# Compressed keys, values and queries as products in three rows, and a different bank for the first compressed scores

## The chip, the cores and the metric

The kernel runs on one core of a Trainium2 chip. The metric is the device time of one execution in microseconds. Before the change it is 561.64 us, the median of three runs (560.61 to 561.91).

## The reference, cut to what matters

One decoder layer: a Conformer convolution module beside native sparse attention, cross-attention, a SwiGLU network, all in float32, 256 positions of width 1024. What the change touches is the compressed branch of the attention:

```
kc = h @ w_in[kc], vc = h @ w_in[vc]          # (S, 4 groups, 64)
q  = h @ w_in[q]                              # (S, 16 heads, 64)
z  = blocks(kc) + pos                         # blocks of 32 positions, stride 16: 15 of them
k_cmp = silu(einsum("bnlgd,lde->bnge", z, w1)) @ w2
s_c   = q . k_cmp * scale + bias              # masked softmax over the 15 blocks
```

The sum over `l, d` is linear, so the positions' own share, `einsum(pos, w1)`, is one vector of 64 numbers that is the same for every block and group. `v_cmp` is made in the same way from `vc`. Beside it, a depthwise convolution with 31 taps runs over 1024 channels.

## The kernel before, in words

Weights come from DRAM in chunks of 128 x 8 x 256 floats, each in two halves of 128 x 1024, in the order u0 to u7, kc, vc, q0 to q3, ks, kw, vs, vw, ga0 to ga3, gc0 and so on. There are two ways to multiply with a chunk.

`gemm` (line 250) splits each half of the weights in two with `split` (line 170): ACT copies it to a rounded high part (line 174), and DVE subtracts that from it to get the low part (line 175). PE then makes three products for each block (`rows`, line 228): high weights by high activations, high by low, low by high, in this order, each a row of eight matmuls. So a half needs its high part first and its low part only for the third row. The raw half lies in one of four buffers ("w"), the high part in one of five, the low part in one of five. `whole` (line 260) takes the raw float32 weights and the float32 activations `hf` in one float32 matmul for each block; the profile shows each of these as two records. Before the change kc, vc and q0 to q3 go through `whole`, and the chunks around them through `gemm`.

The convolution's taps are dealt to DVE (`taps_v`, line 394, with sums in the two PSUM buffers called "pt") and to ACT with POOL (`taps_g`, line 409: ACT multiplies into one of four "vw" buffers, POOL adds to `yt`). They are given low priority (line 437) and fill in between the other work. The last taps on DVE write `part67`, and only then are the two "pt" buffers free.

Tile's scheduler writes the final order of every engine's queue at build time. On the chip each engine takes its own queue strictly in that order.

PSUM has the tags "mm" (two buffers), "s" (two), "pt" (two), "o" and "s0". `bank` (line 136) deals chunks to "mm" and "s" in turn. `compressed_scores` (line 673) makes the compressed scores of the two halves of the queries, `cs_ps0` and `cs_ps1`, four heads at a time between the rows of ga1 and ga2, both in "pt"; DVE then adds them to the bias `nsc` (line 682). `scores` (line 707) makes the selected and window scores of two heads: `s1_0` and `s1_1` in "s", `s0_0` in "s0".

For the compressed keys, ACT copies kc out of PSUM into `kvt` (lines 497 to 500, four copies), DVE gathers the blocks and adds the positions into `zins` (line 504), and 32 matmuls reduce `zins` with `w1t` into `z_ps` (line 523), which a sigmoid and two products finish (lines 526 to 534).

Of the kernel before, what the change touches and what calls it, by code (L numbers as in the profile page):

```python
# [97 lines left out]
def tile_hybrid_block(  # L98
# [161 lines left out]
    def whole(name, x):  # L260

        ps = bank(f"ps_{name}")
        for i in range(2):
            w = raw(name, i)
            for k in range(4):
                kb = 4 * i + k
                for b in range(2):
# [1 line left out]
                    mm = nc.tensor.matmul(ps[:, b], lhsT=w[:, k, cs], rhs=x[:, kb], start=kb + b == 0, stop=kb == NB - 1 and b == 1)  # L269
# [221 lines left out]
    nc.vector.memset(zz, 0.0)
    kvt = long("kvt", 11, (P, 2, GROUPS, S))
    zins = long("zins", 13, (P, 2, 16, GROUPS, 16))
    for kv, name in enumerate(("kc", "vc")):
        ps = whole(name, hf)
# [4 lines left out]
        act = nc.scalar.activation(kc[64:128, 1::2, 0:S - 1], ps[64:128, :, 1:S], AF.Copy)  # L500
# [3 lines left out]
        vec = nc.vector.tensor_tensor(
            out=zin[:, :, :, 0:NCMP],
            in0=bass.AP(tensor=view.tensor, offset=view.offset,
                        ap=[list(view.ap[0]), [2, 16], [S, GROUPS], [16, NCMP]]),
            in1=ppt[:, PP_POS + 16 * kv:PP_POS + 16 * kv + 16].unsqueeze(2).unsqueeze(3).to_broadcast(
                [P, 16, GROUPS, NCMP]), op=ALU.add)
# [7 lines left out]
    def hidden():  # L517


        z_ps = aux("z_ps", [P, 64], "o", 1)  # L520
        for l in range(16):
            for kv in range(2):
                nc.tensor.matmul(z_ps[HD * kv:HD * kv + HD], lhsT=w1t[:, kv, l], rhs=zins[:, kv, l].rearrange("p g n -> p (g n)"),
                                 start=l == 0, stop=l == 15)
# [12 lines left out]

# [135 lines left out]
    def compressed_scores():  # L673

        for qb in range(2):
            cs_ps = aux(f"cs_ps{qb}", [P, HEADS, 2, 16], "pt", 2)
            for hd in range(HEADS):
                with in_line():
                    last[:] = [nc.tensor.matmul(cs_ps[:, hd], lhsT=qh(hd, qb), rhs=kcp[:, hd // 4], start=True, stop=True)]
                yield  # L680
            for i in range(2):
                nc.vector.tensor_tensor(out=nsc[:, qb], in0=cs_ps[:, :, i], in1=nsc[:, qb], op=ALU.add)
# [739 lines left out]
```

## Time and profile before

| | |
|---|---|
| median of three runs | 561.64 us |
| profiled execution | 561.33 us |
| its span | 559.4 us |
| PE busy | 549.5 us, 98% |
| PE weight loads busy | 506.4 us, 91% |
| DVE busy | 458.6 us, 82% |
| ACT busy | 377.3 us, 67% |
| POOL busy | 135.5 us, 24% |
| mean granted TensorE clock | 0.996 |

Shares over the whole span hide the stages. POOL works only from 46 to 172 us, where the convolution runs, and for short pieces later. What bounds a stage is read from that stage's rows: which engine has no idle time, and which wait ends last. All times below are from the span's start; 1.93 us of the execution lie outside the span.

### The profile page before, as it was taken

To read this page: it belongs to the slowest core of one execution; us is meant where nothing else is said; L and a number is where in the kernel's file an instruction comes from. 1 tells how busy PE (TensorE), PEld (TensorE's weight loads), DVE (VectorE), ACT (ScalarE), POOL (GpSimd) and SP (SyncE) were. 2 spreads that over 40 slices of the span, in tenths; PEclk is the share of its full clock that TensorE was granted. 3 is DMA by queue.
4 is the path that set the end of the run, shared out by engine and by line. 5 is a ranking of instruction groups with operands and counts; after the bars stand their busy time and mean duration, and the time that the engine had idled before them with its cause. 6 is when DMAs were issued, how large, how long until landed. Compare 5 with 4: busy or idle time off the path is not lost.

```text
span 559.4 us, 10351 instructions
## 1 busy us (share of the span) xinstructions
PE 549.5 (98%) x3880; PEld 506.4 (91%) x3880; DVE 458.6 (82%) x862; ACT 377.3 (67%) x711; POOL 135.5 (24%) x121
## 2 busy tenths in 40 slices
PE   9999999999989999999999999999999999999995
PEld 8999998899979999899999999999888888888884
DVE  3898976899988799795777866486999999899896
ACT  4678648789866688679745675476576666666653
POOL 0006996989992000300002200060000000000000
PEclk9999999999989999999999999999999999999999
DMA  8949714448453544425555742543654665454531
GB/s 307 392 157 337 254 15 123 133 161 267 155 190 103 167 154 131 136 77 163 180 193 179 262 153 77 189 151 117 224 187 158 199 198 197 151 168 173 197 104 75
DMA packets 29153, 97.30 MB, mean 174 GB/s; under 512 B 3120, under 2 KB 5680, under 8 KB 28848
## 3 DMA queue, kind: packets, MB, share of 16 engines
q1 hardware_dynamic: 28384, 95.42, 50.8%
q10 hardware_dynamic: 720, 1.23, 0.6%
q8 instruction: 30, 0.49, 0.4%
q14 instruction: 19, 0.16, 0.1%
HBM read 95.39 MB, written 1.25 MB: 173 GB/s over the span
## 4 chain that ended last, share of the span: by engine, by line
PE 92%; DVE 5%; ACT 1%; issue 1%; DMA 1%; DVEq 0%
PE ps_f L1148 15%; PE ps_u L239 8%; PE ps_f L1150 7%; PE fo L1180 7%; PE ps_q L269 4%; PE ps_pw L239 4%; PE ps_v L239 4%; PE ps_xq L239 4%; PE ps_wo L239 4%; PE ps_xo L239 4%; PE ps_gc L239 4%; PE ps_ga L239 3%; PE ps_k L239 3%; PE m L1180 3%; PE s L718 2%; PE pt_a L763 1%
## 5 line engine op out<-in xcount | busy, mean ns | idle before, releaser
L421 POOL TENSOR_TENSOR yt<-yt,vw 128x512 f32<-128x512 f32 x61 | 94.1, 1544 | 54.9 <-ACT vw L419 51.3
L1148 PE MATMUL ps_f<-g,f_1h 128*128 128x512 f32 x176 | 49.0, 397 | 0.0
L419 ACT ACTIVATE vw<-vt,ppt 128x256 f32<-128x256 f32 x104 | 44.5, 498 | 6.4 <-POOL yt L421 6.3
L1148 PE MATMUL ps_f<-g,f_0h 128*128 128x512 f32 x176 | 48.5, 397 | 0.0
L405 DVE SCALAR_TENSOR_TENSOR yp<-vt,ppt,yp 128x256 f32<-128x256 f32 x108 | 44.3, 480 | 0.2
L1148 PEld LDWEIGHTS ps_f<-g,f_1h 128*128 128x128 f32 x176 | 32.9, 188 | 7.5
L1148 PEld LDWEIGHTS ps_f<-g,f_0h 128*128 128x128 f32 x176 | 30.1, 188 | 4.1
L175 DVE TENSOR_TENSOR f_1l<-f,f_1h 128x1024 fp32r<-128x1024 f32 x22 | 27.5, 1248 | 4.1 <-ACT f_1h L174 2.6
L1150 PEld LDWEIGHTS ps_f<-g,f_0l 128*128 128x128 f32 x176 | 27.0, 189 | 3.8
L269 PE MATMUL ps_q<-hf,q 128*128 128x256 f32 x128 | 28.5, 381 | 0.0
L1150 PE MATMUL ps_f<-g,f_0l 128*128 128x256 f32 x176 | 28.3, 283 | 0.0
L174 ACT ACTIVATE f_1h<-f 128x1024 fp32r<-128x1024 f32 x22 | 23.3, 1057 | 7.4 <-PE ps_xo L239 3.7
L175 DVE TENSOR_TENSOR f_0l<-f,f_0h 128x1024 fp32r<-128x1024 f32 x22 | 26.8, 1218 | 1.7 <-ACT f_0h L174 1.7
L269 PEld LDWEIGHTS ps_q<-hf,q 128*128 128x128 f32 x128 | 24.1, 190 | 3.2
L1150 PE MATMUL ps_f<-g,f_1l 128*128 128x256 f32 x176 | 26.5, 281 | 0.0
L174 ACT ACTIVATE f_0h<-f 128x1024 fp32r<-128x1024 f32 x22 | 23.1, 1050 | 1.3 <-PE ps_xo L239 1.3
L738 ACT ACTIVATE p<-p,mins 128x256 f32<-128x256 f32 x32 | 15.9, 499 | 11.2 <-DVE mins L723 11.2
L1150 PEld LDWEIGHTS ps_f<-g,f_1l 128*128 128x128 f32 x176 | 23.3, 188 | 0.0
L1151 ACT ACTIVATE ab<-ps_f 128x256 f32<-128x256 f32 x44 | 16.5, 375 | 8.7 <-PE ps_f L1150 7.9
L1152 DVE TENSOR_TENSOR ab<-ps_f,ab 128x256 f32<-128x256 f32 x44 | 18.3, 419 | 4.7 <-ACT ab L1151 4.5
L283 ACT ACTIVATE uh<-sl 128x256 fp32r<-128x256 f32 x22 | 9.1, 415 | 15.8 <-DVE sl L1156 15.8
L1155 ACT ACTIVATE sl<-ab 128x256 f32<-128x256 f32 x22 | 9.2, 417 | 13.5 <-DVE ab L1153 13.0
(574 smaller groups left out, 1608.8 us busy)
## 6 DMA issues: line engine op xcount, KB each, us to landing
f<-in_wst_dram SPq DMA_DIRECT2D x44, 512.0 KB, 5.5
fo<-in_wfo_dram SPq DMA_DIRECT2D x22, 512.0 KB, 3.7
u<-in_wst_dram SPq DMA_DIRECT2D x14, 512.0 KB, 5.6
q<-in_wst_dram SPq DMA_DIRECT2D x8, 512.0 KB, 5.4
ga<-in_wst_dram SPq DMA_DIRECT2D x8, 512.0 KB, 4.2
gc<-in_wst_dram SPq DMA_DIRECT2D x8, 512.0 KB, 4.5
v<-in_wst_dram SPq DMA_DIRECT2D x8, 512.0 KB, 4.7
pw<-in_wst_dram SPq DMA_DIRECT2D x8, 512.0 KB, 3.8
```

Source lines behind the costliest of these rows:

```text
L174: copy = nc.scalar.activation(hi, w, AF.Copy)
L175: splits[name] = copy, nc.vector.tensor_tensor(out=lo, in0=w, in1=f(hi[:]), op=ALU.subtract)
L239: mm = nc.tensor.matmul(ps[:, b], lhsT=lhsT, rhs=rhs, start=row + b + kb == 0, stop=kb == NB - 1 and row == 2 and b == 1)
L269: mm = nc.tensor.matmul(ps[:, b], lhsT=w[:, k, cs], rhs=x[:, kb], start=kb + b == 0, stop=kb == NB - 1 and b == 1)
L405: nc.vector.scalar_tensor_tensor(out=out[:, i] if t == ts[-1] else acc[i], in0=v, scalar=w, in1=acc[i], op0=ALU.mult, op1=ALU.add)
L419: nc.scalar.activation(pr[:, i], v, AF.Identity, scale=w, bias=col(PP_DB, j + i) if t == 0 else 0.0)
L421: nc.gpsimd.tensor_tensor(out=y, in0=y, in1=pr, op=ALU.add)
L1148: nc.tensor.matmul(ps, lhsT=hs[kb // 4][0][:, kb % 4, cs], rhs=fg[:, :, kb], start=kb == 0, stop=False)
L1150: nc.tensor.matmul(ps[:, 1], lhsT=hs[kb // 4][1][:, kb % 4, cs], rhs=fg[:, 0, kb], start=False, stop=kb == NB - 1)
L1151: nc.scalar.activation(ab[:, b], ps[:, 0], AF.Copy)
L1152: nc.vector.tensor_tensor(out=ab[:, b], in0=ps[:, 1], in1=ab[:, b], op=ALU.add)
L1180: mm = nc.tensor.matmul(o, lhsT=a[x], rhs=b[w], start=start and n == 0, stop=stop and n == 2)
```

## The change

The chunks kc, vc and q0 to q3 go through `gemm` in place of `whole`. kc and vc are kept in two tiles of five groups: four hold the keys or values, the fifth is zero except for the sixteen positions of a sub-row, which DVE copies there. The 32 matmuls read the blocks straight out of these tiles with a stride of 16 positions, 75 columns (5 groups by 15 blocks) where they were 64. The fifth group's column is the positions' share; ACT copies it to `at`, and it enters as the sigmoid's bias and as a scalar in the two products. `zins` is gone. `cs_ps0` lies in "s", `cs_ps1` stays in "pt".

```diff
-    in_order = CHUNKS[CHUNK_AT["ks"]:CHUNK_AT["pw0"]]
+    in_order = CHUNKS[CHUNK_AT["kc"]:CHUNK_AT["pw0"]]
...
-    kvt = long("kvt", 11, (P, 2, GROUPS, S))
-    zins = long("zins", 13, (P, 2, 16, GROUPS, 16))
+    kvt = [long(f"{n}t", slot, (P, GROUPS + 1, S)) for n, slot in (("k", 11), ("v", 13))]
     for kv, name in enumerate(("kc", "vc")):
-        ps = whole(name, hf)
-        kc = kvt[:, kv]
-        nc.scalar.activation(kc[0:64, 0::2, :], ps[0:64], AF.Copy)
...
-        zin = zins[:, kv]
-        nc.vector.memset(zin[:, :, :, NCMP:], 0.0)
-        view = kc
-        vec = nc.vector.tensor_tensor(
-            out=zin[:, :, :, 0:NCMP],
-            in0=bass.AP(tensor=view.tensor, offset=view.offset,
-                        ap=[list(view.ap[0]), [2, 16], [S, GROUPS], [16, NCMP]]),
-            in1=ppt[:, PP_POS + 16 * kv:PP_POS + 16 * kv + 16].unsqueeze(2).unsqueeze(3).to_broadcast(
-                [P, 16, GROUPS, NCMP]), op=ALU.add)
+        ps = gemm(name, h)
+        kc = kvt[kv]
+        nc.scalar.activation(kc[0:64, 0:GROUPS:2, :], ps[0:64], AF.Copy)
...
+        nc.vector.memset(kc[:, GROUPS], 0.0)
+        vec = nc.vector.tensor_copy(kc[:, GROUPS, 0:32:2], ppt[:, PP_POS + 16 * kv:PP_POS + 16 * kv + 16])
         convolve(10 - 2 * kv, 5, act, vec)
...
-        z_ps = aux("z_ps", [P, 64], "o", 1)
+        z_ps = aux("z_ps", [P, GROUPS + 1, NCMP], "o", 1)
         for l in range(16):
             for kv in range(2):
-                nc.tensor.matmul(z_ps[HD * kv:HD * kv + HD], lhsT=w1t[:, kv, l], rhs=zins[:, kv, l].rearrange("p g n -> p (g n)"),
+                nc.tensor.matmul(z_ps[HD * kv:HD * kv + HD], lhsT=w1t[:, kv, l], rhs=kvt[kv][:, :, 2 * l:2 * l + 16 * (NCMP - 1) + 1:16],
                                  start=l == 0, stop=l == 15)
-        zs = small("zs", [P, 64], tag="zs", bufs=2)
-        sig = nc.scalar.activation(zs, z_ps, AF.Sigmoid)
+        zs = small("zs", [P, GROUPS, NCMP], tag="zs", bufs=2)
+        at = small("at", [P, 1])
+        nc.scalar.activation(at, z_ps[:, GROUPS, 0:1], AF.Copy)
+        sig = nc.scalar.activation(zs, z_ps[:, :GROUPS], AF.Sigmoid, bias=at)
...
-        nc.vector.tensor_tensor(out=zz[:HD, 0, :64], in0=z_ps[:HD], in1=zs[:HD], op=ALU.mult)
-        nc.vector.tensor_tensor(out=zs[HD:], in0=z_ps[HD:], in1=zs[HD:], op=ALU.mult)
+        nc.vector.scalar_tensor_tensor(out=z1, in0=z_ps[:HD, :GROUPS], scalar=at[:HD], in1=zs[:HD], op0=ALU.add, op1=ALU.mult)
+        nc.vector.scalar_tensor_tensor(out=zs[HD:], in0=z_ps[HD:, :GROUPS], scalar=at[HD:], in1=zs[HD:], op0=ALU.add, op1=ALU.mult)
...
     for j in range(4):
-        ps = whole(f"q{j}", hf)
+        ps = gemm(f"q{j}", h)
...
-            cs_ps = aux(f"cs_ps{qb}", [P, HEADS, 2, 16], "pt", 2)
+            cs_ps = aux(f"cs_ps{qb}", [P, HEADS, 2, 16], ("s", "pt")[qb], 2)
```

The scheduler's order moves with it, from the chunk u7 to the first scores; behind these the queues of all engines hold the same instructions in the same order as before. Three places matter. Line numbers of the changed kernel are smaller by up to 8 behind line 489.

On DVE, in the stage of u5: the twelve new low parts (kc_0l to q3_1l, "0" and "1" the two halves) are set between the convolution's taps (`yp`), the first of them here.

```order
 L405 SCALAR_TENSOR_TENSOR yp_726<-vt_352,ppt,yp_726 128x256
 L405 SCALAR_TENSOR_TENSOR yp_727<-vt_352,ppt,yp_727 128x256
+L175 TENSOR_TENSOR kc_0l<-kc_1049,kc_0h 128x1024
 L449 TENSOR_TENSOR vt_353<-ps_u_752,sg_813 128x256
 L405 SCALAR_TENSOR_TENSOR yp_726<-vt_352,ppt,yp_726 128x256
```

A low part now stands ahead of the gated input `vt` of the convolution; the number of taps on DVE is what it was.

On ACT, in the stages of u5 to u7: the twelve new high parts (kc_0h and so on) stand between the products `vw` that ACT makes for POOL.

```order
 L419 ACTIVATE vw_15_836<-vt_351,ppt 128x256 x2
+L174 ACTIVATE kc_1h<-kc_1079 128x1024
+L174 ACTIVATE vc_0h<-vcw 128x1024
 L448 ACTIVATE sg_901<-ps_u_840 128x256
 L419 ACTIVATE vw_16_914<-vt_351,ppt 128x256 x2
 L419 ACTIVATE vw_18_922<-vt_351,ppt 128x256 x2
+L174 ACTIVATE vc_1h<-vcw 128x1024
 L419 ACTIVATE vw_19_926<-vt_351,ppt 128x256 x2
+L174 ACTIVATE q_0h<-q_0_1239 128x1024
 L448 ACTIVATE sg_991<-ps_u_930 128x256
```

Each `vw` waits until POOL has taken the one four before it, and the high part behind it waits along.

On PE, from the last compressed scores ahead of the first selected scores to the first row of ga2. Before:

```order
L679 MATMUL cs_ps1_1910<-kcp_1154,qt_1157 128x32 x4
L695 MATMUL gt_ps_1932<-cpt_67,sgn_1766 128x48 x2
L718 MATMUL s1_0_1946<-kdh_1433,qt_1157 128x512
L718 MATMUL s1_0_1946<-kdl_1434,qt_1157 128x512
L720 MATMUL s0_0_1944<-kdh_1433,qt_1157 128x256
L720 MATMUL s0_0_1944<-kdl_1434,qt_1157 128x256
L718 MATMUL s1_1_1954<-kdh_1433,qt_1157 128x512
L718 MATMUL s1_1_1954<-kdl_1434,qt_1157 128x512
```

Now:

```order
L712 MATMUL s1_0_2188<-kdh_1675,qt_1237 128x512
L712 MATMUL s1_0_2188<-kdl_1676,qt_1237 128x512
L714 MATMUL s0_0_2186<-kdh_1675,qt_1237 128x256
L714 MATMUL s0_0_2186<-kdl_1676,qt_1237 128x256
L714 MATMUL s0_0_2186<-kdh_1675,qt_1237 128x256
L714 MATMUL s0_0_2186<-kdl_1676,qt_1237 128x256
L239 MATMUL ps_ga2_2208<-hh_86,ga2_0h_2211 128x256 x8
L673 MATMUL cs_ps1_2152<-kcp_1234,qt_1237 128x32
L712 MATMUL s1_1_2196<-kdh_1675,qt_1237 128x512
L712 MATMUL s1_1_2196<-kdl_1676,qt_1237 128x512
L673 MATMUL cs_ps1_2152<-kcp_1234,qt_1237 128x32 x3
L239 MATMUL ps_ga2_2208<-hl_87,ga2_0h_2211 128x256 x8
```

`s1_1` is set behind the first row of ga2, since it takes the "s" buffer that `cs_ps0` had. That buffer is free when DVE has added `cs_ps0` to the bias for the second time, which stands there so:

```order
L405 SCALAR_TENSOR_TENSOR part67_361<-vt3_354,ppt_66,yp7_1314 128x256
L175 TENSOR_TENSOR ga2_1l_2283<-ga2_1_2280,ga2_1h_2282 128x1024
L175 TENSOR_TENSOR ga3_0l_2315<-ga3_0_2312,ga3_0h_2314 128x1024
L676 TENSOR_TENSOR nsc_1027<-cs_ps0_2095,nsc_1027 128x256
L175 TENSOR_TENSOR ga3_1l_2345<-ga3_1_2342,ga3_1h_2344 128x1024
L676 TENSOR_TENSOR nsc_1027<-cs_ps0_2095,nsc_1027 128x256
```

Three low parts stand between the last tap and that second addition.

More of the change, by code (lines that the diff above doesn't have):

```diff
@@ L491, in tile_hybrid_block @@
     nc.vector.memset(zz, 0.0)
-    kvt = long("kvt", 11, (P, 2, GROUPS, S))
-    zins = long("zins", 13, (P, 2, 16, GROUPS, 16))
+    kvt = [long(f"{n}t", slot, (P, GROUPS + 1, S)) for n, slot in (("k", 11), ("v", 13))]
     for kv, name in enumerate(("kc", "vc")):
-        ps = whole(name, hf)
-        kc = kvt[:, kv]
-        nc.scalar.activation(kc[0:64, 0::2, :], ps[0:64], AF.Copy)
-        nc.scalar.activation(kc[64:128, 0::2, 0:S - 1], ps[0:64, :, 1:S], AF.Copy)
-        nc.scalar.activation(kc[0:64, 1::2, :], ps[64:128], AF.Copy)
-        act = nc.scalar.activation(kc[64:128, 1::2, 0:S - 1], ps[64:128, :, 1:S], AF.Copy)
-        zin = zins[:, kv]
-        nc.vector.memset(zin[:, :, :, NCMP:], 0.0)
-        view = kc
-        vec = nc.vector.tensor_tensor(
-            out=zin[:, :, :, 0:NCMP],
-            in0=bass.AP(tensor=view.tensor, offset=view.offset,
-                        ap=[list(view.ap[0]), [2, 16], [S, GROUPS], [16, NCMP]]),
-            in1=ppt[:, PP_POS + 16 * kv:PP_POS + 16 * kv + 16].unsqueeze(2).unsqueeze(3).to_broadcast(
-                [P, 16, GROUPS, NCMP]), op=ALU.add)
+        ps = gemm(name, h)
+        kc = kvt[kv]
+        nc.scalar.activation(kc[0:64, 0:GROUPS:2, :], ps[0:64], AF.Copy)
+        nc.scalar.activation(kc[64:128, 0:GROUPS:2, 0:S - 1], ps[0:64, :, 1:S], AF.Copy)
+        nc.scalar.activation(kc[0:64, 1:GROUPS:2, :], ps[64:128], AF.Copy)
+        act = nc.scalar.activation(kc[64:128, 1:GROUPS:2, 0:S - 1], ps[64:128, :, 1:S], AF.Copy)
+        nc.vector.memset(kc[:, GROUPS], 0.0)
+        vec = nc.vector.tensor_copy(kc[:, GROUPS, 0:32:2], ppt[:, PP_POS + 16 * kv:PP_POS + 16 * kv + 16])
         convolve(10 - 2 * kv, 5, act, vec)
@@ L517, in hidden @@
     def hidden():
-        z_ps = aux("z_ps", [P, 64], "o", 1)
+        z_ps = aux("z_ps", [P, GROUPS + 1, NCMP], "o", 1)
         for l in range(16):
             for kv in range(2):
-                nc.tensor.matmul(z_ps[HD * kv:HD * kv + HD], lhsT=w1t[:, kv, l], rhs=zins[:, kv, l].rearrange("p g n -> p (g n)"),
+                nc.tensor.matmul(z_ps[HD * kv:HD * kv + HD], lhsT=w1t[:, kv, l], rhs=kvt[kv][:, :, 2 * l:2 * l + 16 * (NCMP - 1) + 1:16],
                                  start=l == 0, stop=l == 15)
-        zs = small("zs", [P, 64], tag="zs", bufs=2)
-        sig = nc.scalar.activation(zs, z_ps, AF.Sigmoid)
+        zs = small("zs", [P, GROUPS, NCMP], tag="zs", bufs=2)
+        at = small("at", [P, 1])
+        nc.scalar.activation(at, z_ps[:, GROUPS, 0:1], AF.Copy)
+        sig = nc.scalar.activation(zs, z_ps[:, :GROUPS], AF.Sigmoid, bias=at)
         with behind(sig):
             nc.scalar.activation(small("exps", [P, 1]), eps1, AF.Exp)
-        nc.vector.tensor_tensor(out=zz[:HD, 0, :64], in0=z_ps[:HD], in1=zs[:HD], op=ALU.mult)
-        nc.vector.tensor_tensor(out=zs[HD:], in0=z_ps[HD:], in1=zs[HD:], op=ALU.mult)
-        nc.vector.tensor_copy(
-            zz[HD:, 1].rearrange("p (g r n) -> p g r n", g=GROUPS, r=4),
-            zs[HD:].rearrange("p (g n) -> p g n", g=GROUPS).unsqueeze(2).to_broadcast([HD, GROUPS, 4, 16]))
+        z1 = zz[:HD, 0, :64].rearrange("p (g n) -> p g n", g=GROUPS)[:, :, 0:NCMP]
+        nc.vector.scalar_tensor_tensor(out=z1, in0=z_ps[:HD, :GROUPS], scalar=at[:HD], in1=zs[:HD], op0=ALU.add, op1=ALU.mult)
+        nc.vector.scalar_tensor_tensor(out=zs[HD:], in0=z_ps[HD:, :GROUPS], scalar=at[HD:], in1=zs[HD:], op0=ALU.add, op1=ALU.mult)
+        nc.vector.tensor_copy(zz[HD:, 1].rearrange("p (g r n) -> p g r n", g=GROUPS, r=4)[:, :, :, 0:NCMP],
+                              zs[HD:].unsqueeze(2).to_broadcast([HD, GROUPS, 4, NCMP]))
     def compressed():
```

## The prediction

> **What bounds the kernel now.** I read the chain of waits first, then the waits themselves, then the stage around the change. The chain (shares of the span) says PE:
>
> ```profile
> PE 92%; DVE 5%; ACT 1%; issue 1%; DMA 1%; DVEq 0%
> ```
>
> So time taken from PE should count one for one, unless PE gets a new wait. In the stage that changes, from the last split of u7 to the last tap, the engines' busy times are (PE, PE loads, DVE, ACT, POOL; then clock and DMA share):
>
> ```profile
> core 0: us, PE busy (x) PEld busy (x) DVE busy (x) ACT busy (x) POOL busy (x), PEclk, DMA share, GB/s
> 66.20:157.60 91.40, 88.71 (x631) 81.71 (x629) 79.33 (x142) 73.06 (x150) 82.78 (x64) 1.00 0.45 143
> ```
>
> PE leads here, but DVE has only 12.1 us of idle time and POOL 8.6. PE's one wait of any size, and what surrounds it (start, length, then the idle time ahead in brackets):
>
> ```profile
> PE cs_ps L679 <- DVE part L405: 2.8, 1, 2.8
> ...
> 157.67 0.62 PE L679 MATMUL cs_ps<-kcp,qt 128*128 128x32 f32 x4 [2.76 <-DVE part L405]
> 158.13 1.58 PE L239 MATMUL ps_ga<-hl,ga_0h 128*128 128x256 f32 x8
> ...
> 162.07 0.55 PE L679 MATMUL cs_ps<-kcp,qt 128*128 128x32 f32 x4
> 162.47 1.19 PE L239 MATMUL ps_ga<-hh,ga_1h 128*128 128x256 f32 x8
> ...
> 164.88 0.51 PE L679 MATMUL cs_ps<-kcp,qt 128*128 128x32 f32 x4
> ...
> 168.56 1.10 PE L239 MATMUL ps_ga<-hh,ga_0h 128*128 128x256 f32 x8
> ...
> 180.80 0.40 PE L718 MATMUL s<-kdh,qt 128*128 128x512 f32 x1
> ```
>
> The first compressed scores wait until DVE's taps let go of "pt". After that wait the clock is low:
>
> ```profile
> 159.00:160.00 1.00, 1.00 (x7) 1.00 (x6) 1.00 (x1) 1.00 (x2) 1.00 (x2) 0.50 0.57 180
> ```
>
> Two pairs of a row and four scores took 3.94 us from 158.13 to 162.07, the next two 2.41 us from 162.47 to 164.88: the dip costs 1.5 us, 1.6 with the slower first scores. So DVE's last tap already sets PE's pace here, and costs 2.8 + 1.6 = 4.4 us.
>
> **The change on PE.** A chunk by the float32 way and one by three rows:
>
> ```profile
> 85.78 6.91 PE ps_vc L269 x32
> ...
> 304.90 5.68 PE ps_wo L239 x48
> ```
>
> Six chunks save 6 x 1.23 = 7.4 us. The 32 matmuls of z grow from 64 to 75 columns:
>
> ```profile
> 100.41 2.08 PE L523 MATMUL z_ps<-zins,w1t 128*64 128x64 f32 x62
> ```
>
> 2.08 x 75/64 = 2.44, so +0.4 us. No row shows a float32 stream with a stride of 64 bytes; below it could be free (+0.4), above I let it double (+2.8). I take +0.4, since the nearest row has the same matmul, and PE is not the bound just there, as the DVE sum will show. Left alone, PE would be 7.0 us early, and 11.4 with the wait gone.
>
> **The change on DVE.** It loses two gathers and gains twelve subtractions of 128x1024. The gathers, and the subtraction where POOL is idle (last stages), then by window where POOL works (busy time and count):
>
> ```profile
> L504 DVE TENSOR_TENSOR zins<-kvt,ppt 128x960 f32<-128x960 f32 x2 | 4.6, 2308 | 6.9 <-ACT kvt L500 6.9
> ...
> L175 DVE TENSOR_TENSOR f_0l<-f,f_0h x22: 1208/1218/1226, 358.3 to 480.4; 128x1024 fp32r<-128x1024 f32 x22
> ...
> 46.00:66.20 20.20, 10.58 (x7) 1.00 0.90 334
> 117.00:157.60 40.60, 23.84 (x13) 1.00 0.60 198
> ```
>
> Beside POOL one takes 10.58/7 = 1.51 and 23.84/13 = 1.83 us, against 1.22 alone. I take the mean of the twenty, 34.42/20 = 1.72, as the new ones lie between these two windows: 12 x 1.72 = 20.6 us. The end of the last tap follows from the queue, anchored at the end of u7's last subtraction:
>
> ```profile
> 64.48 1.80 DVE L175 TENSOR_TENSOR u_1l<-u,u_1h 128x1024 fp32r<-128x1024 f32 x1
> 66.20 0.87 DVE L405 SCALAR_TENSOR_TENSOR yp<-vt,ppt,yp 128x256 f32<-128x256 f32 x2
> ...
> 157.14 0.86 DVE L405 SCALAR_TENSOR_TENSOR part<-vt,ppt,yp 128x256 f32<-128x256 f32 x2
> ```
>
> 66.2 + (79.33 - 4.62) + 20.6 = 161.5 us with no idle at all. Idle time: the 6.9 us on the copies of kc and vc go, as nothing on DVE reads them. What remains is waiting for ACT's high parts. At four places (vc_1h, q0_0h, q0_1h and q1_1h) they stand behind `vw` products that wait for POOL. I put 1.5 us (0 to 4). The last tap's first buffer is then free at T = **163.0** us, against 157.6 before. **DVE becomes the bound**: at 7.0 us early PE would issue cs_ps1 at about 153 us, ten us ahead of T, and so it waits for low parts from ks on. That wait hides the 7.4 us saved and any stride in z.
>
> **From T on.** `cs_ps0` no longer needs "pt", but `cs_ps1` does, nine rows on in the queue. So the wait moves and is not removed: queued behind it are ga1's last row, the gates' transposes, `scores(0)` and ga2. Before, 164.88 to 180.80 = 15.92 us pass from cs_ps1 to the second `scores`, by the same instructions. PE reaches cs_ps1 about 4.1 us after ga1's low part is ready, which is some 7 us ahead of T in DVE's queue; the idle piece is then about 3 us, like the 2.76, and I charge the dip again, 1.6 us. **A new wait**: s1_1 needs the buffer of `cs_ps0`, so two additions with three subtractions around them behind the last tap. The nearest rows:
>
> ```profile
> L175 DVE TENSOR_TENSOR ga_0l<-ga,ga_0h x4: 1210/2118/2309, 142.2 to 160.3; 128x1024 fp32r<-128x1024 f32 x4
> ...
> 164.78 0.87 DVE L682 TENSOR_TENSOR nsc<-cs_ps,nsc 128x256 f32<-128x256 f32 x2
> ```
>
> T + 0.4 + 3 x 1.83 + 0.87 = T + 6.8. PE arrives there at T + 4.3 (164.88 to 168.56, less s1_1, plus a row of ga2) + 1.6 = T + 5.9: 0.9 us of wait (0 to 2, by 1.21 and 2.31 a subtraction). Second `scores` at T + 15.92 + 1.6 + 0.9 = T + 18.4 = 181.4, against 180.80: **+0.6 us**. Behind that both queues are the same and PE is the bound again, with DVE's lateness, at most the 5.4 us of the last tap, taken up by its idle time (1.7 of 14.1 and 4.6 of 20 us):
>
> ```profile
> 157.60:171.70 14.10, 14.03 (x103) 13.87 (x104) 12.44 (x25) 7.09 (x15) 13.82 (x9) 0.88 0.60 196
> 180.00:200.00 20.00, 20.00 (x167) 18.78 (x166) 15.37 (x53) 15.24 (x45) 0.00 (x0) 1.00 0.41 128
> ```
>
> If that cover failed, up to 5.4 us would come on top.
>
> **Costed at nothing**, with what hides it: the twelve high parts on ACT (1.04 us each by the row here, 12.5) go into ACT's 91.40 - 73.06 = 18.3 us of idle time; without it they would stand ahead of the low parts one for one. The two memsets and copies of the fifth group, below 0.5 us each by the memset row here, stand in the stage of u0 and u1, where DVE idles 36.20 - 32.77 = 3.4 us:
>
> ```profile
> L174 ACT ACTIVATE ga_0h<-ga 128x1024 fp32r<-128x1024 f32 x4 | 4.2, 1044 | 0.0
> ...
> 78.20 0.48 DVE L491 MEMSET zz<- 128x512 f32 x1
> ...
> 30.00:66.20 36.20, 36.20 (x308) 36.20 (x307) 32.77 (x49) 26.29 (x44) 19.07 (x14) 1.00 0.76 273
> ```
>
> The copy to `at` and the two products with it replace instructions of the same size. On SP's queue the halves of q1 and q2 are issued earlier; their buffers come free when DVE has split the half four before and no longer when PE has used it. They have 5.4 us to land and four low parts, some 14 us, to do it in:
>
> ```profile
> q<-in_wst_dram SPq DMA_DIRECT2D x8, 512.0 KB, 5.4
> ```
>
> [...] Subtractions read two operands from SBUF; beside POOL they take 1.51 to 1.83 us, and POOL's additions 2.27 where they take 1.27 alone. [...]
>
> **The rivals.** (1) *PE's saving counts in full*: the low parts hide, as the chain's 92% suggests. Then 11.4 us go: 549.9. Against it: DVE's 161.5 us without idle time is already behind PE. (2) *The subtractions are cheap*, because scattered between taps they seldom meet an addition. At 1.22 us T is 66.2 + 74.7 + 14.6 = 155.5, or -6.9 us: 554.4. For it: the window of u, 1.51; against: POOL is busy 82.78 of 91.40 us. (3) *POOL falls behind, and ACT's high parts with it* (slower). POOL's rows (idle time ahead in brackets):
>
> ```profile
> 84.62 1.27 POOL L425 TENSOR_TENSOR yt<-yt,part 128x512 f32<-128x512 f32 x1
> 90.21 2.62 POOL L421 TENSOR_TENSOR yt<-yt,vw 128x512 f32<-128x512 f32 x2 [4.32 <-ACT vw L419]
> ...
> 120.19 8.45 POOL L421 TENSOR_TENSOR yt<-yt,vw 128x512 f32<-128x512 f32 x5 [1.06 <-ACT vw L419]
> ...
> 141.75 12.07 POOL L421 TENSOR_TENSOR yt<-yt,vw 128x512 f32<-128x512 f32 x7
> ...
> 161.51 2.27 POOL L425 TENSOR_TENSOR yt<-yt,part 128x512 f32<-128x512 f32 x1
> ```
>
> Twelve subtractions that each cost POOL 1.22 us make it 14.6 late, less its idle 5.4: 9.3. The place that decides is ga3_0h, now behind the `vw` of tap 28, which waits until POOL has added tap 24's: the fifth of the seven at 141.75, so 150.4 before and 159.7 then. ACT needs two us more, 161.6, and DVE wants it at T + 2.2 = 165.2. So it costs nothing up to 12.9 us of lateness, 1.5 us a subtraction. At 1.9 us POOL is 17.4 late, and the second `scores` 4.5 later: 561.33 + 0.6 + 4.5 = 566.4.
>
> **How the numbers follow.** The forecast is that DVE's queue takes PE's place and the time hardly moves: 561.33 + 0.6 = 561.9 for the profiled execution, whose own time is 0.3 under the median, so **562.2** us. Its own range: 1.51 with 0.5 of idle gives T = 159.5 and -2.9, 1.83 with 3 us gives T = 165.9 and +3.5; so 559 to 566. A measurement of this kernel can tell about 0.2%, 1.1 us, from no change. Chances: forecast 0.68 (faster 0.15, same 0.31, slower 0.22), rival 1 0.05, rival 2 0.13, rival 3 0.14. Together faster 0.33, same 0.31, slower 0.36. The range of 558 to 566.4 holds the forecast's and ends at rival 3's; it leaves out rival 1 and most of 2.
>
> **What would show it.** In the changed profile: a chunk of q at 5.7 us where it does not wait; DVE without idle pieces from 90 us to the last tap at about 163; PE waiting on low parts (L175) of ks to ga1, then at cs_ps1 on `part`, with a clock below 0.9 just after, then some at s1_1. It is wrong if the subtractions average under 1.5 us, if DVE idles over 4 us for ACT, or if PE passes cs_ps1 without a wait.

## The result, and the profile after

The changed kernel takes 559.0 us, the median of 13 runs (558.45 to 560.21), against 563.1 us (560.61 to 565.0) for the kernel before in 13 runs beside it. The ratio is 0.9942, with a 95% interval of 0.9926 to 0.9957: faster by 0.6%, where I had forecast a time that hardly moves (+0.6 us). The 559.0 us lie in my range of 558 to 566.4, near its lower end; the direction was missed. The profiled executions differ by 561.33 - 558.7 = 2.6 us; why the medians differ by 4.1 is told below, with the clock.

The chain of waits, by engine, is no longer PE's almost alone (92% before):

```profile
PE 74%; POOL 15%; ACT 5%; DVE 4%; issue 3%; POOLq 0%; ACTq 0%
```

The share that PE lost went to POOL and not to DVE. From 51 to 165 us the chain runs through POOL's additions for the convolution, with ACT's rows in between from 85 to 108 us, and it comes back to PE over ACT's high part of gc0 and DVE's low part of it. DVE and POOL are about equally full in that stage; the window of the prediction again, now:

```profile
66.20:157.60 91.40, 87.80 (x756) 85.32 (x755) 88.97 (x146) 80.36 (x156) 88.16 (x59) 1.00 0.46 142
```

DVE is idle for 2.4 us there and POOL for 3.2. No run below takes work from POOL alone, so which of the two holds the other back is open.

PE's waits (total, times, longest) are other ones than I forecast. None is on a low part (L175), and none is at the compressed scores:

```profile
PE vc_ps L538 <- DVE zz L527: 1.3, 1, 1.3
PE cb_ps L469 <- DVE vt L449: 1.2, 1, 1.2
PE kc_ps L533 <- DVE zz L525: 1.1, 1, 1.1
...
PE ps_f L1142 <- DVE ab L1146: 0.5, 1, 0.5
PE ps_gc L239 <- ACT sga L647: 0.3, 1, 0.3
```

The rows of PE that answer to those shown of before (start, length):

```profile
82.56 2.02 PE L469 MATMUL cb_ps<-tables 128*128 128x48 f32 x16 [1.22 <-DVE vt L449]
...
99.67 0.33 PE L515 MATMUL z_ps<-vt,w1t 128*64 128x75 f32 x1
...
103.98 0.39 PE L239 MATMUL ps_q<-hl,q_0h 128*128 128x256 f32 x1
...
119.06 0.43 PE L533 MATMUL kc_ps<-zz,ppt 128*128 128x64 f32 x2 [1.09 <-DVE zz L525]
123.56 0.63 PE L538 MATMUL vc_ps<-ppt,zz 128*128 128x64 f32 x4 [1.29 <-DVE zz L527]
...
153.32 1.11 PE L239 MATMUL ps_ga<-hh,ga_0h 128*128 128x256 f32 x8
154.27 0.51 PE L673 MATMUL cs_ps<-kcp,qt 128*128 128x32 f32 x4
...
159.92 0.62 PE L673 MATMUL cs_ps<-kcp,qt 128*128 128x32 f32 x4
...
164.51 0.47 PE L712 MATMUL s<-kdh,qt 128*128 128x512 f32 x1
...
176.24 0.40 PE L712 MATMUL s<-kdh,qt 128*128 128x512 f32 x1
178.14 1.22 PE L239 MATMUL ps_gc<-hh,gc_0h 128*128 128x256 f32 x8 [0.35 <-ACT sga L647]
```

The first row of ga1 starts at 153.32 us. Before it stood here:

```profile
153.80 1.10 PE L239 MATMUL ps_ga<-hh,ga_0h 128*128 128x256 f32 x8
```

So six chunks in three rows, worth 7.4 us of PE's time, have left 0.5 us. The whole visible gain arises after that: `cs_ps0` no longer waits 2.76 us, the clock does not dip, `cs_ps1` at 159.92 does not wait either, and the second `scores` start 4.6 us earlier than before (180.80). At the end of the span 2.6 of them are left.

How late DVE is shows at the first product `zz`, for which PE waits at `kc_ps`; first before, when PE came to `kc_ps` 9 us later (115.90 us), then now:

```profile
106.85 0.21 DVE L530 TENSOR_TENSOR zz<-z_ps,zs 64x64 f32<-64x64 f32 x1
```

```profile
118.74 0.27 DVE L525 SCALAR_TENSOR_TENSOR zz<-z_ps,at,zs 64x60 f32<-64x60 f32 x1
```

DVE's subtractions by window (busy time and count), and the end of its taps:

```profile
46.00:66.20 20.20, 11.28 (x7) 1.00 0.92 344
66.20:90.00 23.80, 11.64 (x7) 1.00 0.35 100
90.00:117.00 27.00, 11.10 (x7) 1.00 0.51 156
117.00:160.00 43.00, 19.59 (x12) 1.00 0.50 162
...
159.40 0.86 DVE L405 SCALAR_TENSOR_TENSOR part<-vt,ppt,yp 128x256 f32<-128x256 f32 x2
```

The first "pt" buffer is free at about 159.85 us, half of the last row. PE, at 159.92, comes there in the same tenth of a microsecond.

Where the rest of the gain went is seen one stage later. The rows there (idle time in brackets), and behind them POOL's last fold before the change:

```profile
165.58 0.91 ACT L419 ACTIVATE vw<-vt,ppt 128x256 f32<-128x256 f32 x2 [2.87 <-POOL yt L421]
167.47 1.66 DVE L175 TENSOR_TENSOR gc_0l<-gc,gc_0h 128x1024 fp32r<-128x1024 f32 x1 [3.10 <-ACT gc_0h L174]
...
177.22 1.68 POOL L292 TENSOR_TENSOR ysum<-ysum 128x256 f32<-128x256 f32 x1
```

```profile
170.93 0.73 POOL L292 TENSOR_TENSOR ysum<-ysum 128x256 f32<-128x256 f32 x1
```

POOL makes its last fold of the convolution (L292) at 177.22 us, 6.3 us later than before. One of ACT's products for it waits 2.87 us, the high part of gc0 behind that, and DVE behind that for 3.10 us.

### The profile page after: what moved, and what is told of

It is laid out like the page before. It is cut to its first block, busy times and chain, and to the rows that moved or that the text cites. A ratio compares the mean times of both kernels' runs of the same rounds, so it can differ in the third digit from the quotient of the medians.

```text
span 556.8 us, 10583 instructions
## 1 busy us (share of the span) xinstructions
PE 545.0 (98%) x3976; PEld 505.2 (91%) x3976; DVE 470.0 (84%) x874; ACT 388.1 (70%) x724; POOL 147.6 (27%) x121
## 4 chain that ended last, share of the span: by engine, by line
PE 74%; POOL 15%; ACT 5%; DVE 4%; issue 3%; POOLq 0%; ACTq 0%
PE ps_f L1142 15%; POOL yt L421 13%; PE ps_f L1144 7%; PE fo L1174 7%; PE ps_pw L239 4%; PE ps_v L239 4%; PE ps_xq L239 4%; PE ps_wo L239 4%; PE ps_xo L239 4%; PE ps_gc L239 3%; PE ps_k L239 3%; PE m L1174 3%; PE ps_u L239 3%; ACT vw L419 2%; POOL vw L417 2%
## 5 line engine op out<-in xcount | busy, mean ns | idle before, releaser
L421 POOL TENSOR_TENSOR yt<-yt,vw 128x512 f32<-128x512 f32 x61 | 101.1, 1658 | 49.9 <-DMA u<-in_wst_dram 46.3
L175 DVE TENSOR_TENSOR f_1l<-f,f_1h 128x1024 fp32r<-128x1024 f32 x22 | 27.5, 1248 | 4.4 <-ACT f_1h L174 2.5
L175 DVE TENSOR_TENSOR f_0l<-f,f_0h 128x1024 fp32r<-128x1024 f32 x22 | 26.8, 1219 | 1.7 <-ACT f_0h L174 1.7
L417 POOL TENSOR_SCALAR vw<-vt,ppt 128x256 f32<-128x256 f32 x18 | 17.1, 964 | 0.5
```

The costliest lines, as they stand in the source:

```text
L175: splits[name] = copy, nc.vector.tensor_tensor(out=lo, in0=w, in1=f(hi[:]), op=ALU.subtract)
L417: nc.gpsimd.tensor_scalar(out=pr[:, i], in0=v, scalar1=w, scalar2=0.0, op0=ALU.mult, op1=ALU.add)
L421: nc.gpsimd.tensor_tensor(out=y, in0=y, in1=pr, op=ALU.add)
```

## The experiments

Theory A says that the bank's move brings the gain and the products in three rows bring nothing. The rivals are that the rows bring it (B), that the stride of z limits it (C), and, where PE's time alone would count, E; theory D and the others are stated with the runs that test them. All times are medians. The kernel before is timed anew beside each set, and its median moved from 561.4 to 563.8 us between the sets, so kernels of different sets are compared by their ratios and by their traces.

### One part alone

`bank_only` is the kernel before with only

```diff
-            cs_ps = aux(f"cs_ps{qb}", [P, HEADS, 2, 16], "pt", 2)
+            cs_ps = aux(f"cs_ps{qb}", [P, HEADS, 2, 16], ("s", "pt")[qb], 2)
```

> The kernel before with one edit: cs_ps0 in "s", cs_ps1 in "pt". Theory A (the gain of the whole change is the wait and the clock dip at cs_ps0, 2.76 + 1.6 = 4.4 us, and the products in three rows only made the bank's move keep its worth): PE passes cs_ps0 at about 154.9 us without a wait or a dip and reaches cs_ps1 at 160.5, behind the last tap's 157.6, so no wait there. DVE's queue does not move, so the second addition of cs_ps0 still ends at 165.65; PE now reaches s1_1 at 167.86 - 4.4 = 163.5 and waits 2.2 us there. Second scores at 178.6 us (180.80 before, 176.24 in the changed kernel), time 2.2 us under the kernel before, about 0.4%. Rival B (the three rows bring the gain): the wait only moves from cs_ps0 to cs_ps1 or s1_1, second scores at 180 or later, time within 1 us of before.

`no_bank` is the changed kernel with that line undone.

> The changed kernel with the bank's move undone: both compressed scores in "pt". Theory A: PE comes to cs_ps0 at 154.3 us and the last tap frees "pt" at 159.9, so it waits 5.6 us there and the clock dips behind it for 1.6 us or more; cs_ps1 then has no wait. Second scores at 176.24 + 7 = 183 us, time 5 to 7 us over the changed kernel, 564 to 566, slower than before. Rival B (the three rows bring the gain): second scores below 179 us, time 559 to 561.

| kernel | median | before | ratio | second `scores` |
|---|---|---|---|---|
| bank_only | 560.99 | 561.43 | 0.9980 (0.9966 to 0.9995) | 181.00 |
| no_bank | 567.27 | 561.43 | 1.0077 (1.0052 to 1.0102) | 186.48 |

Neither part is worth much alone, and the three rows alone make the kernel slower. PE in `no_bank`, at `cs_ps0` and at the second `scores`:

```profile
159.52 1.03 PE L673 MATMUL cs_ps<-kcp,qt 128*128 128x32 f32 x4 [5.13 <-DVE part L405]
...
186.48 0.40 PE L712 MATMUL s<-kdh,qt 128*128 128x512 f32 x1
```

`bank_only` passes `cs_ps0` and `cs_ps1` without a wait, and then waits where theory A had put it, for the length it had named. PE and DVE there:

```profile
163.27 0.47 PE L718 MATMUL s<-kdh,qt 128*128 128x512 f32 x1
...
166.42 0.47 PE L718 MATMUL s<-kdh,qt 128*128 128x512 f32 x1 [2.22 <-DVE nsc L682]
...
181.00 0.40 PE L718 MATMUL s<-kdh,qt 128*128 128x512 f32 x1
```

```profile
160.96 2.30 DVE L175 TENSOR_TENSOR ga_0l<-ga,ga_0h 128x1024 fp32r<-128x1024 f32 x1
163.18 2.31 DVE L175 TENSOR_TENSOR ga_1l<-ga,ga_1h 128x1024 fp32r<-128x1024 f32 x1
165.41 0.87 DVE L682 TENSOR_TENSOR nsc<-cs_ps,nsc 128x256 f32<-128x256 f32 x2
```

`s1_1` needs the buffer of `cs_ps0`, and the additions that free it (L682) stand behind three low parts in DVE's queue. What I had left out of the expectation is that this wait, too, is followed by a dip of the clock: from `s1_1` to the second `scores` 14.58 us pass, and 12.94 before. So 4.4 us were won and 2.2 + 1.6 given back; PE was also 0.8 us later at ga1 in this execution (154.56), and the second `scores` are no earlier than before (180.80). The 178.6 expected were missed.

In `no_bank` the wait of 5.13 us is close to the 5.6 expected, but the dip behind it is four times as long as I had priced it, hence 186.48 in place of 183, and 567.3 us in place of 564 to 566.

### The additions moved

`bank_nsc` is `bank_only` with DVE's two additions of `cs_ps0` ahead of the three low parts:

```diff
-            splits[name] = copy, nc.vector.tensor_tensor(out=lo, in0=w, in1=f(hi[:]), op=ALU.subtract)
+            with behind(*low_first.get(name, ())):
+                splits[name] = copy, nc.vector.tensor_tensor(out=lo, in0=w, in1=f(hi[:]), op=ALU.subtract)
...
-                nc.vector.tensor_tensor(out=nsc[:, qb], in0=cs_ps[:, :, i], in1=nsc[:, qb], op=ALU.add)
+                add = nc.vector.tensor_tensor(out=nsc[:, qb], in0=cs_ps[:, :, i], in1=nsc[:, qb], op=ALU.add)
+            if qb == 0:
+                low_first.update({n: (add,) for n in ("ga2_1", "ga3_0", "ga3_1")})
```

> The kernel before with cs_ps0 in "s", and DVE's two additions of cs_ps0 (nsc) set right behind the last tap, ahead of the three low parts of ga2 and ga3. With the bank alone PE waited 2.22 us at s1_1 for these additions and the clock dipped behind it (s1_1 to the second scores 14.58 us in place of 12.94, so 1.64). Theory F (the bank's move is worth 4.4 us, and the place of the additions in DVE's queue decides whether it is kept): no wait at s1_1, no dip, second scores at 181.00 - 3.9 = 177.1, time 3.9 us under bank_only, about 557.3 and 0.7% under the kernel before. Rival G (the wait moves on again, to the low part of ga2 that is now 0.9 us later): second scores at 179 or later, time within 2 us of before.

`after_nsc` is the changed kernel with this edit.

> The changed kernel with the additions of cs_ps0 right behind the last tap, and nothing else. In the changed kernel PE hardly waits at s1_1 (0.1 us), as the scheduler set it one row later. Theory F: nothing to gain, second scores at 176.2, time within 0.5 us of the changed kernel (559.0). If it gains 2 us or more, the place of the additions had cost there too.

| kernel | median | before | ratio | second `scores` |
|---|---|---|---|---|
| bank_nsc | 557.02 | 562.99 | 0.9903 (0.9881 to 0.9925) | 176.55 |
| after_nsc | 559.40 | 562.99 | 0.9940 (0.9919 to 0.9961) | 176.32 |

`bank_nsc` has none of the change's products in three rows, no strided z, and is 2.4 us faster than the changed kernel with the same edit, and 1.0% faster than the kernel before. In its stage PE has no wait left:

```profile
155.07 0.51 PE L680 MATMUL cs_ps<-kcp,qt 128*128 128x32 f32 x4
...
160.63 0.51 PE L680 MATMUL cs_ps<-kcp,qt 128*128 128x32 f32 x4
...
163.60 0.40 PE L721 MATMUL s<-kdh,qt 128*128 128x512 f32 x1
...
176.55 0.40 PE L721 MATMUL s<-kdh,qt 128*128 128x512 f32 x1
```

So the gain is the removed wait, with its dip. In the changed kernel the additions cost nothing, as expected: `after_nsc` has its ratio (0.9940 against 0.9942), though its profiled execution has a dip of one piece at 85 us, behind a wait of 1.03 us at `cb_ps` (two rows of eight matmuls take 1.87 and 1.91 us there, and 1.11 in the changed kernel). In the changed kernel the scheduler had set `s1_1` one row later, and the three low parts behind the last tap took 1.21 to 1.24 us each and not 2.3. It seems that POOL waited there instead: a pair of its products took 4.15 us beside them, and the same pair 0.94 in `after_nsc`, where two of the three low parts take 2.3 us.

```profile
160.14 4.15 POOL L417 TENSOR_SCALAR vw<-vt,ppt 128x256 f32<-128x256 f32 x2
```

Why it fell to POOL in one kernel and to DVE in the other was not tested. What the rows cost against `bank_nsc` shows row by row between the two traces: PE in the changed kernel is 0.8 us earlier at `cs_ps0` and 0.3 at the second `scores`, and then 0.3 later in gc0 (behind the wait on `sga`), 1.1 later from 194 us on, and 1.7 later behind the wait on `ab` at 485 us.

### Which rows

`gemm_q` is the changed kernel with kc and vc through `whole`; `gemm_q_nsc` has the additions moved as well, and `gemm_kv_nsc` is the complement.

```diff
-        ps = gemm(name, h)
+        ps = whole(name, hf)
         kc = kvt[kv]
```

> The changed kernel with kc and vc back in one float32 product each, and q0 to q3 in three rows. PE gets 2 x 1.23 = 2.5 us more, DVE loses the four subtractions of kc and vc (1.52 + 1.90 + 1.92 + 2.10 = 7.4 us). Theory D (in the changed kernel DVE's lateness, through the gated input vt and the products zz in its queue, eats the PE time that is saved): the waits of cb_ps on vt (1.2) and of kc_ps and vc_ps on zz (2.4) go, the last tap is at about 153 us, PE reaches cs_ps1 at about 159 without a wait, and the second scores at 175 to 175.5; time 1 us under the changed kernel, about 558. Rival E (PE's time counts one for one): PE 2.5 us later throughout, second scores at 178.7, time 561.

> The changed kernel with kc and vc in one float32 product each, and the additions of cs_ps0 right behind the last tap. Without the second edit PE came to cs_ps0 at 152.0 us, 2.2 earlier than in the changed kernel, and then waited 6.54 us at s1_1 for the additions; from s1_1 to the second scores it took 14.96 us in place of 12.94. Theory F: that wait and 2.0 us of dip go, second scores at 182.23 - 8.5 = 173.7, span 552.2, time about 554.5, 1.2% under the kernel before and 0.8% under the changed one. Rival H (behind the convolution ACT or POOL are late by the same amount, so that the gated ga stage or gc waits): second scores by 174, but time 557 or more, no better than bank_nsc.

> The complement: kc and vc in three rows, q0 to q3 in one float32 product each, cs_ps0 in "s", its additions right behind the last tap. PE gets 4 x 1.23 = 4.9 us more than in the changed kernel, DVE loses eight subtractions (12.3 us). Theory D (DVE's lateness eats PE's saving): the waits on zz (2.4 us) go, that of cb_ps on vt (1.2) stays, as the low parts of kc still stand ahead of vt; PE at cs_ps1 at 162.4 without a wait, second scores at 178.7, time about 561, some 7 us over gemm_q_nsc. Rival E (PE's time counts one for one): second scores at 181.1, time 563.5.

| kernel | median | before | ratio | second `scores` |
|---|---|---|---|---|
| gemm_q | 563.13 | 561.43 | 1.0028 (1.0011 to 1.0045) | 182.23 |
| gemm_q_nsc | 556.48 | 562.99 | 0.9888 (0.9863 to 0.9914) | 174.47 |
| gemm_kv_nsc | 558.17 | 562.99 | 0.9923 (0.9894 to 0.9952) | 176.78 |

In `gemm_q` the first half of theory D holds: the waits on `vt` and `zz` are gone and PE comes to `cs_ps0` at 152.0 us, 2.2 us earlier than in the changed kernel with all six chunks in rows. The time was missed by 5 us, since all of it and more is lost at `s1_1`. PE, then DVE:

```profile
159.79 0.47 PE L712 MATMUL s<-kdh,qt 128*128 128x512 f32 x1
...
167.27 0.77 PE L712 MATMUL s<-kdh,qt 128*128 128x512 f32 x1 [6.54 <-DVE nsc L676]
```

```profile
160.31 1.61 DVE L175 TENSOR_TENSOR ga_1l<-ga,ga_1h 128x1024 fp32r<-128x1024 f32 x1 [4.90 <-ACT ga_1h L174]
```

The last tap ends at 155.4 us, but the first of the three low parts ahead of the additions then waits 4.90 us for its high part, which ACT makes at 159.24. So more than DVE's own work keeps the additions back: they stand behind the low parts, and the first of these waits for ACT. Why ACT is late was not followed; it had waited 2.8 us for POOL from 147 to 155 us.

With the additions moved, this version is the fastest, 556.48 us (555.23 to 557.22), a little ahead of `bank_nsc` (556.75 to 557.70); the two ranges overlap. The second `scores` come 2.1 us earlier than in `bank_nsc`, 0.8 behind the expected 173.7:

```profile
174.47 0.40 PE L715 MATMUL s<-kdh,qt 128*128 128x512 f32 x1
```

But only 0.7 us reach the end of the span (554.4 against 555.1): rival H, in part. PE waits 0.68 us for `sga` at gc0 and loses 0.7 more in small pieces up to 204 us. With the 0.8 this is why the expected 554.5 was too low.

`gemm_kv_nsc` came out 3 us better than expected, at 558.2. The waits on `zz` are gone and the one on `vt` stays, as theory D said, but I had added the costs to the changed kernel's. Against `bank_nsc` two chunks save 2.5 us, z costs 2.4 more and `cb_ps` waits 0.8 for `vt`, so PE should be 0.7 us later at `cs_ps0`; it is 0.2 later (155.30 against 155.07).

### The stride of z

`contig` keeps every instruction of the changed kernel and reads 15 neighbours in each group, so that it lacks the right positions in z.

```diff
-                nc.tensor.matmul(z_ps[HD * kv:HD * kv + HD], lhsT=w1t[:, kv, l], rhs=kvt[kv][:, :, 2 * l:2 * l + 16 * (NCMP - 1) + 1:16],
+                nc.tensor.matmul(z_ps[HD * kv:HD * kv + HD], lhsT=w1t[:, kv, l], rhs=kvt[kv][:, :, 2 * l:2 * l + NCMP],
```

> The changed kernel with the 32 matmuls of z reading 15 positions next to each other in each group in place of every sixteenth (so z is made of the wrong positions, and the compressed branch with it; the number of columns and every queue's order stay). It prices the stride. Theory A: the pairs of z come at 0.076 us each (0.065 x 75/64) in place of 0.13, so z takes 2.6 us in place of 4.7 and PE is 2.1 us earlier; but kc_ps waits for DVE's products zz at 118.7 us, which stand in DVE's queue and don't move, so the wait there grows from 1.1 to about 3.2 us and the time stays within 0.7 us of the changed kernel. Rival C (the stride costs the time): second scores at 174.1 us, time 2.1 us lower, 556.9. If the pace stays at 0.13 us the stride is not the cause, and the 75 columns in five groups are.

`in_place_nsc` is `gemm_kv_nsc` with `whole` for kc and vc too: no chunk in three rows, the gathers gone, z strided.

> bank_nsc with the positions read in place (five groups, 75 columns at a stride of 16, no gathers on DVE), and kc, vc and q0 to q3 still in one float32 product each. DVE loses 4.6 us of work and the waits for the copies of kc and vc (6.9), which bounds nothing in bank_nsc; z costs PE 4.3 us in place of 2.0 (the pace measured with and without the stride). Theory: where PE alone is the bound the stride counts one for one: second scores at 176.55 + 2.3 = 178.9, time 559.3 against 557.0 of bank_nsc. Rival: DVE's relief shortens some wait that the profile does not show, and the time is that of bank_nsc or lower.

The rows of `contig`:

```profile
98.88 0.28 PE L515 MATMUL z_ps<-vt,w1t 128*64 128x75 f32 x1
...
101.16 0.38 PE L239 MATMUL ps_q<-hl,q_0h 128*128 128x256 f32 x1
...
118.39 0.69 PE L533 MATMUL kc_ps<-zz,ppt 128*128 128x64 f32 x2 [3.23 <-DVE zz L525]
```

The same 62 records take 2.28 us from start to the next chunk's row, and 4.31 in the changed kernel (99.67 to 103.98); before, with 64 columns, it was 2.01. So the eleven columns cost 0.3 us at most and the stride of 64 bytes 2.0. And it costs nothing in the end: the 2.1 us come back as wait at `kc_ps`, 3.23 us where there were 1.09, as expected (3.2). The ratio is 0.9949 (0.9930 to 0.9969), against 0.9942 for the changed kernel, and the second `scores` start at 176.24 us in both. Part of this is the clock: behind the 3.23 us `contig` has a dip of two pieces, which the changed kernel lacks, and which falls in part into the time that PE had waited at `vc_ps`. What `contig` would take without it, no run shows.

Where DVE does not hold PE the stride counts. The second `scores` of `in_place_nsc`:

```profile
178.31 0.40 PE L715 MATMUL s<-kdh,qt 128*128 128x512 f32 x1
```

They are 1.8 us behind `bank_nsc`, where 2.3 were expected, and the time is 558.88 us (ratio 0.9910, 0.9893 to 0.9928). PE has no wait there, so the 4.6 us of gathers that DVE saves buy little: the second `scores` are 0.6 us ahead of the 178.9 expected.

### Do PE and DVE meet at cs_ps1?

If PE and DVE both come to `cs_ps1` at 160 us, then neither alone can be made faster with profit. `late_comp` takes PE's waits on `zz` away, `few_taps` DVE's last taps, `late_few` both, all on `after_nsc`.

```diff
-            elif j == 2:
-                compressed()
...
     ps_kw = gemm("kw", h)
+    with behind(*last):
+        compressed()
```

```diff
-    on_v = chain(taps_v(0, taps[FIRST_G:], part01), taps_v(2, taps, yt[:, 2:4]), taps_v(6, taps[LAST_G:], part67))
+    on_v = chain(taps_v(0, taps[FIRST_G:], part01), taps_v(2, taps, yt[:, 2:4]), taps_v(6, taps[LAST_G:LAST_G + 15], part67))
```

> The changed kernel with the additions of cs_ps0 right behind the last tap (after_nsc), and kc_ps and vc_ps set behind the chunk kw in place of q2, so that PE no longer waits for the products zz (2.2 to 2.4 us in the changed kernel). Theory D (PE and DVE come to cs_ps1 together at 160 us, so PE time saved ahead of it is worth nothing): PE comes to cs_ps1 at 157.9 and now waits 2.2 us there for the last tap, which stays at 160; the clock dips behind it by up to 1.6 us. Second scores at 176.3 to 178, time 0 to 1.6 us over after_nsc (559.4). Rival E (waits on PE cost one for one): second scores at 174.0, time 557.1.

> after_nsc with the last six of the 21 taps that DVE makes for the channel blocks 6 and 7 left out (the convolution of these blocks lacks them), 12 instructions at the end of DVE's tap queue: the last tap comes 4.7 us earlier, at 155.4, and nothing ahead of it moves. Theory D: PE is no earlier at cs_ps1 (160.1), so the second scores stay at 176.1 and the time falls by no more than the wait at pc_ps behind (0 to 1.3 us): 558 to 559.4. Rival I (DVE alone bounds the stage, as was predicted): second scores at 172 to 173, time 555 to 556.

> Both edits together: kc_ps and vc_ps behind kw, and the last six taps of DVE left out. Theory D: only now does PE's time count, as neither the products zz nor the last tap hold it: PE at cs_ps1 at 157.9 without a wait, second scores at 174.0 and time 2.2 us or more under after_nsc, about 557. If it is no faster than few_taps, something else holds PE there.

The kernel before takes 563.76 us beside these, and beside `in_place_nsc`.

| kernel | median | ratio | second `scores` | PE's waits |
|---|---|---|---|---|
| late_comp | 559.68 | 0.9941 (0.9916 to 0.9966) | 175.14 | `vt` 1.6, `g_ps` 1.9, `nsc` 2.0, `ab` 0.6 |
| few_taps | 560.37 | 0.9931 (0.9908 to 0.9954) | 176.44 | `vt` 1.7, `sga` 0.6, `nsc` 0.9, `ab` 1.5 |
| late_few | 559.88 | 0.9926 (0.9908 to 0.9944) | 174.40 | `vt` 0.6, `g_ps` 1.9, `sga` 1.8, `nsc` 0.9, `ab` 1.7 |

By the ratios none of the three is clear of `after_nsc` (0.9940). That neither edit gains alone is what theory D says; that both together gain 2.2 us, as it also says, did not come, and the place of the waits is another. In `late_comp` PE waits 1.9 us earlier in the queue, at `g_ps`, whose bank `kc_ps` now holds until DVE has read it:

```profile
PE pc_ps L862 <- DVE nsc L829: 2.0, 1, 2.0
PE g_ps L597 <- DVE kcp L285: 1.9, 1, 1.9
PE cb_ps L470 <- DVE vt L450: 1.6, 1, 1.6
```

`few_taps` does not test the point cleanly: a wait of 1.70 us at `cb_ps` was followed by 6.8 us of half clock, so PE came late for another reason. `late_few` has the second `scores` at 174.40, near the expected 174.0, and then loses 1.8 us to `sga` and 0.9 to `nsc`, and 1.7 to `ab` at 485 us; the 557 us expected were missed by 3. By the waits in its trace the one on `sga` seems to lead back to POOL: one of ACT's products waits 3.5 us for POOL, DVE waits 4.0 us for the high part of gc0 behind it, and the softmax ahead of `sga` waits for DVE. So the meeting at `cs_ps1` was one of several: with all six chunks in rows, PE is held at `vt`, at `zz` or `kcp`, at `sga` and at `nsc`, and in these runs, where one wait was taken away, another took its place. That the meeting at 160 us by itself set the time was not shown.

## Why the prediction was wrong, step by step

- **What bounds the kernel** held: the wait at `cs_ps0` and its dip, 4.4 us in that profile. `bank_nsc`, which takes away only that, is faster by more (1.0%). By the mean granted clocks (0.996 in the profiled execution, 0.992 or less in 24 of the 51 runs beside the experiments) the clock would be low for longer in many executions than in the one profiled.
- **PE's saving** held: the rows of vc start at 85.87 us and those of q0 at 91.55 in the changed kernel, 5.68 us for a chunk, by the row quoted.
- **z at +0.4** failed. From 2.27 us in two pieces it went to 4.69, +2.4. I had 0.4 to 2.8 and took the lower end because the nearest row had the same matmul, though it lacked the stride. By `contig`, whose 62 records take 2.28 us where the changed kernel's take 4.31, 2.0 us of the 2.4 are the stride.
- **The DVE sum** was 3.1 us too long: T came at 159.85 and not 163.0. The subtractions from 66 to 160 us took 11.64 + 11.10 + 19.59 = 42.3 us, 1.06 of them for the end of u7's last one. The 25 others took 41.3, 1.65 each; I had 1.83 for the old thirteen and 1.72 for the new twelve, 44.4 in all. This term, 3.1 us too large, turned the sign of the forecast. The remaining differences (a start 1.0 later, 0.9 more of idle time, 2.0 less of other work) cancel.
- **"DVE becomes the bound … it waits for low parts from ks on"** is the step of the mechanism that failed. PE never waited for a low part. It was held earlier, by small results of DVE that stand in the same queue: `vt` (1.22) and `zz` (1.09 and 1.29). Together with the stride these are 5.6 of the 7.0 us that PE was to be early at ga1, where it was early by 0.5; the rest, 0.9, is in pieces that I did not follow. That DVE's queue eats PE's saving was right as far as PE's waits show it; the chain names POOL, and which of the two holds the other is open. That it would do so at the low parts and at `cs_ps1`, where PE would wait for T, was wrong. I had looked only at what the added instructions produce, and not at what else stands behind them in the queue and is awaited by PE.
- **"So the wait moves and is not removed"** failed as a consequence. PE came to `cs_ps1` with T and not ahead of it: no wait, no dip. The 1.6 for the dip and most of the 0.9 at `s1_1` were not paid, T was 3.1 earlier, so the second `scores` came at 176.24 and not 181.4. "PE passes cs_ps1 without a wait" was among the signs of being wrong.
- **"DVE's lateness … taken up by its idle time"** failed in part: 2.0 us were lost from the second `scores` to the end.
- **The size by luck.** My sum with the measured T gives 0.6 - 3.1 = -2.5 us, and the profiled executions differ by 2.6. That is luck: the dip and wait that were not paid (about 2.0 us) and the 2.0 us lost behind the second `scores`, which I had put at nothing, happen to cancel.
- **The range** has a slip: 3.5 us over before is 565, not 566.
- **Rival 3's mechanism** was there in small: POOL 6.3 us late, ACT's product and the high part behind it late by 2.87 us. It decided at gc0 and not at ga3, and cost 0.35 us of wait there. The same kind of wait, for a high part that ACT makes late, is 4.90 us long in `gemm_q`, and POOL's additions are on the chain from 51 to 165 us. That each of the twelve subtractions costs POOL its own 1.22 us was my estimate, and no run shows it: POOL was busy 147.6 us in all where it had been busy 135.5, about 1.0 us for each. I gave this rival too small a part.
- Rivals 1 and 2 were not what happened: PE's saving left 0.5 of 7.0 us, and T at 159.85 is nearer to my value than to 155.5, though only by 1.2 us.

## What to carry to other kernels

When work is added to a queue, list everything that stands behind it in that queue and is awaited by the bound engine, small results above all; the first of them that becomes late can be the new wait. A bank moved to free one wait binds whatever used that bank next: check where the instruction that frees it stands in its queue, and what those ahead of it wait for on other engines, since two additions set ahead of three low parts made the difference between a ratio of 0.998 and one of 0.990 here (`bank_only` and `bank_nsc`). A wait on PE cost more than its length here where the clock fell behind it (2.22 us and 1.6 more in `bank_only`), and by the mean granted clocks of the kernel before (0.987 to 0.999 in 51 runs) the amount varies between executions.
